# Bidirectional HGRN2 keys from the middle of each chunk, projections and heads in another order, two weight chunks loaded earlier

## The chip, the cores and the metric

The kernel runs on one core of one Trainium2 chip. The metric is the device time of one execution in microseconds (us), median of the runs. TensorE multiplies matrices (PE in the profile, PEld its weight loads), VectorE (DVE) and ScalarE (ACT) work on tiles of 128 partitions, GpSimd (POOL) does little here, and SyncE (SP) only issues DMA transfers.

## What is computed

One encoder layer for 256 tokens of width 1024, in float32: a token mixer, a layer norm, a mixture of 32 experts (top 4 per token), a second layer norm. All weights are read from DRAM once; the experts' are 32 x 12 MB. The change lies in the mixer's recurrence, which runs forwards and backwards over chunks of 32 tokens:

```python
b = jnp.cumsum(logf, axis=3)
b_ref = b[:, :, :, CHUNK // 2 - 1:CHUNK // 2]
b_last = b[:, :, :, CHUNK - 1:CHUNK]
scores = jnp.einsum('bhntd,bhnsd->bhnts', q * jnp.exp(b - b_ref), k * jnp.exp(b_ref - b))
...
kv = jnp.einsum('bhnsd,bhnse->bhnde', k * jnp.exp(b_last - b), v)
decay = jnp.exp(b_last[:, :, :, 0])
def step(S, inp):
    kv_c, dec_c = inp
    return dec_c[..., None] * S + kv_c, S
...
o_inter = jnp.einsum('bhntd,bhnde->bhnte', q * jnp.exp(b), S_prev)
```

## The kernel before

**Steps.** The mixer's matrix products are cut into 64 steps (`run`): 48 for the input projection (24 column blocks of 256, two steps of half the depth each), 8 for the two branch matrices, 8 for the output matrix. A step first splits the weights of the step after next into a rounded copy (`hi`, ScalarE, L233) and the rest (`lo`, VectorE, L234), orders the chunk that comes due (`load_on`), then issues two halves of TensorE work, three groups of four matmuls each (L176: hi, low activations with hi, lo). The copies have three buffers, so a split waits for the step three back. `after` functions (sigmoids, copies of a projection's result) run in the next step.

**Tasks.** What is not a projection is written as generators in `tasks`, each with a first step, and is advanced once in each half step (or in each n-th). `factors(p)` makes, for a pair of heads p, the cumulated decays (`dec`) and from them `qt` and `kt` (queries and keys measured from the chunk's middle), `kd` (keys measured from the chunk's end) and `xx` (queries times the whole decay). `head(h)` makes the scores from `kt` and `qt` (L378), transposes `kd` (L383, `ktp`), copies that to SBUF on ScalarE (L387), multiplies it with the values (L399, `kvp`), runs the recurrence over 8 chunks on VectorE (L409, L412), and sums up on TensorE (L417, L422, `o`); then it normalises (L427 to L434), transposes (L438, `ytp`) and multiplies with the gate. `biases()` splits the experts' biases into three bf16 parts (L514 to L519). Four engines and SP run in the order written (`manual_schedule`), so the place of a task in the steps fixes what stands behind what.

**Chunks.** Weights come in chunks of 1 MB into a ring of slots: pools b (9 slots), c (4), a (4), d (4). The mixer's own chunks use the four a slots. Its intermediate tiles lie in b and c slots (`hold`, `hold_c`), and pool d takes the room of the mixer's operand tiles and is made when they are given up (`mix_ctx.close()`, after the last product with the output matrix). `PF` lists the steps at which a chunk of the first two experts is ordered ahead, one per slot of the ring in turn: 14 in all. After the mixer SP orders every further chunk as its slot falls free. SP works its orders in turn, so one that waits holds up those behind it.

Of the kernel before, what the change touches and what calls it, by code (L numbers as in the profile page):

```python
# [18 lines left out]
P = 128  # L19
T = 256  # L20
# [20 lines left out]
def encoder(ctx: ExitStack, tc: tile.TileContext, x, w_in, conv_w, p_a, lbl, norm_w, p_b, w_o, ln1_g, ln1_b,  # L41
# [136 lines left out]
    def two_parts(hi, lo, src):  # L178
# [6 lines left out]
    cc = hold_c[0][:, 0:512].rearrange("p (i t) -> p i t", i=2)  # L185
    z = hold_c[0][:, 512:1028].rearrange("p (i t) -> p i t", i=2)
    dgs = hold_c[0][:, 1028:1540].rearrange("p (i n e) -> p i n e", i=2, n=NT)
    qT, gwT = (hold_c[1][:, i * 1024:(i + 1) * 1024].rearrange("p (h t) -> p h t", h=NH) for i in range(2))
    sg = [hold_c[2 + q // 2][:, q % 2 * 1024:(q % 2 + 1) * 1024].rearrange("p (i n t) -> p i n t", i=2, n=2)
          for q in range(4)]  # L190
# [3 lines left out]
    xx0, sig1, omf, qt, kt, kd, sig0, lf = [dirs(*n) for n in ((1, 0), (1, 1), (2, 0), (4, 0), (4, 1), (5, 0), (8, 0),  # L194
                                                              (8, 1))]
    sig, xxs = [sig0, sig1], [xx0, sig0]
    dec = half_of(2, 1).rearrange("p (d t) -> p d t", d=2)
    kns = half_of(5, 1).rearrange("p (i d n e) -> p i d n e", i=2, d=2, n=NT)
    Ss = [hold[6 + i].rearrange("p (d c e) -> p d c e", d=2, c=NCH) for i in range(2)]
# [3 lines left out]
    nc.gpsimd.memset(dgs, 0.0)  # L203
    mxh = mxl = None
# [33 lines left out]
    ahead, PF = [], [8, 26, 31, 32, 35, 36, 40, 41, 42, 47, 47, 53, 58, 58]  # L238
# [84 lines left out]
    def factors(p):  # L323
# [23 lines left out]
        blast = bass.AP(tensor=dec.tensor, offset=dec.offset + CH - 1, ap=[p0, [2 * T - CH + 1, 2], [CH, nchk], [0, CH]])  # L347
# [3 lines left out]
        nc.vector.tensor_tensor(four(xx), b4, bref, op=OP.subtract)  # L351
        yield
        nc.vector.tensor_tensor(four(kd), blast, b4, op=OP.subtract)
        yield
        qb = qT[:, None, 2 * p:2 * p + 2, :].to_broadcast([P, 2, 2, T])
        nc.scalar.activation(flat(qt), flat(xx), AF.Exp)
        yield
        nc.scalar.activation(flat(kt), flat(xx), AF.Exp, scale=-1.0)
        nc.vector.tensor_mul(qt, qt, qb)
        yield  # L360
        nc.scalar.activation(flat(kd), flat(kd), AF.Exp)
        nc.vector.tensor_mul(kt, kt, omf)
        yield
        nc.scalar.activation(flat(lf), dec.rearrange("p d t -> p (d t)"), AF.Exp)
        nc.vector.tensor_mul(kd, kd, omf)
        yield
        nc.vector.tensor_mul(xx, lf, qb)
        yield

    def head(h):  # L370
        p, h2 = h // 2, h % 2
        v, qp, eb, dg, kn, S, yb = vs[:, p], xxs[p], lf, dgs[:, h2], kns[:, h2], Ss[h2], ybs[h2]
# [8 lines left out]
        for d in range(2):  # L381
            for tt in range(NT):
                nc.tensor.transpose(kv4[:, d, tt, :], kd[:, d, h2, tt * P:(tt + 1) * P], ident)  # L383
# [18 lines left out]
        for i in range(2):  # L402
            for n in range(4 * i, min(4 * i + 4, NCH - 1)):
                for d in range(2):
# [3 lines left out]
                    if n == 0:  # L408
                        nc.scalar.copy(S[:, d, c + step, :], kv)  # L409
                    else:  # L410
                        last = c * CH + (CH - 1 if d == 0 else 0)
                        nc.vector.scalar_tensor_tensor(S[:, d, c + step, :], S[:, d, c, :],  # L412
                                                       eb[:, d, h2, last:last + 1], kv, op0=OP.mult, op1=OP.add)
            yield
        o = bank("b", "o")[:, 0:NT * P].rearrange("p (n e) -> p n e", n=NT)
# [84 lines left out]
    def biases():  # L500

        def load(src):
            bf = half_of(3, len(bfs) % 2)[0:96]
# [84 lines left out]

    for p in range(2):
# [4 lines left out]
        if p == 0:  # L594
            project(3584, got_g(0))
            project(512, got_c(0))
    project(1024, got_h(0))
    project(0, got_b(0))
    project(512 + H2, got_c(1))
    project(1024 + H2, got_h(1))  # L600
    project(H2, got_b(1))
    project(3584 + H2, got_g(1))
    for q in range(4):
        for i in range(2):
            project(4096 + i * DM + q * H2, got_gate(q, i))
# [602 lines left out]
```

## Time and profile before

| | us |
|---|---|
| median of 3 runs | 1169.03 (1168.68 to 1171.88) |
| the profiled execution | 1167.09, its span 1165.4 |
| TensorE busy in the span | 1074.9 (92%) |
| VectorE busy | 343.8 (30%) |
| ScalarE busy | 224.5 (19%) |
| bytes moved by DMA | 440.39 MB, mean 378 GB/s |

The span is cut by the program into a mixer (to about 227 us), the experts, and a short end. Busy shares are averages over these and say little for one of them; the views by stretch do.

### The profile page before, as it was taken

Reading aid. Unit: us, or ns where it says so; the run is one execution under the profiler, and the core shown is the slowest. Engines: PE = TensorE matmul, PEld = TensorE weight load, DVE = VectorE, ACT = ScalarE, POOL = GpSimd, SP = SyncE. Lnnn points to the kernel's source line nnn. Section 1 sums busy time; section 2 is a strip of 40 time slices with the busy share of each in tenths; the row PEclk is TensorE's granted clock in tenths of the full one; section 3 lists DMA queues with packets and bytes.
Section 4 is the critical chain, followed back from the end, with each engine's and each line's share of the span. In section 5 each row is a group of like instructions: output and inputs, shape, how many; then the busy total and the mean of one; then the engine's idle time right before and its main releaser. Section 6 shows DMA issues by size and latency. Waiting matters only on the chain. (4 is left out here: it accounts for less than half of the span.)

```text
span 1165.4 us, 14653 instructions
## 1 busy us (share of the span) xinstructions
PE 1074.9 (92%) x6176; PEld 544.8 (47%) x6176; DVE 343.8 (30%) x631; ACT 224.5 (19%) x376; POOL 12.4 (1%) x36
## 2 busy tenths in 40 slices
PE   8999999989999999999999898989898999888994
PEld 7899899734343443433343333333333333333344
DVE  5678746621212131313212121212121111111124
ACT  4857444311010101010110101010010001010111
POOL 1000000000000000000000000000000000000001
PEclk9999999999999999999999999999999999999998
DMA  9645597699999999999999999999999999999994
GB/s 295 208 146 169 194 363 273 251 416 423 425 422 425 424 424 425 422 424 424 424 424 424 424 423 424 423 423 425 423 425 423 424 424 424 424 424 425 427 378 127
DMA packets 109701, 440.39 MB, mean 378 GB/s; under 512 B 8224, under 2 KB 41184, under 8 KB 76864
## 3 DMA queue, kind: packets, MB, share of 16 engines
q1 hardware_dynamic: 109440, 439.05, 92.9%
q8 instruction: 50, 0.82, 0.3%
q10 hardware_dynamic: 192, 0.36, 0.1%
q14 instruction: 19, 0.16, 0.0%
HBM read 438.34 MB, written 1.05 MB: 377 GB/s over the span
## 5 line engine op out<-in xcount | busy, mean ns | idle before, releaser
L683 PE MATMUL hb<-ck,xg 128*64 128x512 f32 x2048 | 465.3, 603 | 39.3 <-DMA ck<-in_w_dram 39.3
L683 PEld LDWEIGHTS hb<-ck,xg 128*64 128x64 f32 x2048 | 143.0, 138 | 342.7 <-issue 243.2
L915 PE MATMUL y<-ck,aT 128*64 128x512 f32 x960 | 214.0, 598 | 17.5 <-ACT aT L692 17.4
L659 DVE TENSOR_SCALAR g<-hb 128x512 f32<-128x512 f32 x32 | 22.1, 691 | 658.5 <-PE hb L683 658.5
L915 PEld LDWEIGHTS y<-ck,aT 128*64 128x64 f32 x960 | 66.6, 138 | 152.9 <-issue 119.5
L660 ACT ACTIVATE s<-g 128x512 f32<-128x512 f32 x32 | 20.1, 629 | 557.0 <-DVE g L659 557.0
L234 DVE TENSOR_TENSOR lo<-ck,hi 128x1024 fp32r<-128x1024 f32 x62 | 75.4, 1221 | 53.5 <-ACT hi L233 53.2
L233 ACT CAST hi<-ck 128x1024 fp32r<-128x1024 f32 x62 | 64.3, 1044 | 48.1 <-PE pj L176 38.2
L176 PE MATMUL pj<-xh,hi 128*128 128x256 f32 x352 | 60.2, 295 | 0.8 <-ACT hi L233 0.8
L886 PEld LDWEIGHTS gthp<-oneh,xs 128*128 128x128 f32 x480 | 54.7, 192 | 12.8 <-PE hb L683 8.1
L176 PE MATMUL pj<-xh,lo 128*128 128x256 f32 x352 | 58.5, 290 | 2.0 <-DVE lo L234 2.0
L176 PE MATMUL pj<-xl,hi 128*128 128x256 f32 x352 | 58.6, 290 | 0.0
L927 PE MATMUL cb<-ys,gT 128*128 128x512 f32 x120 | 57.8, 605 | 0.0
L886 PE MATMUL gthp<-oneh,xs 128*128 128x128 f32 x480 | 57.6, 278 | 0.0
L176 PEld LDWEIGHTS pj<-xh,lo 128*128 128x128 f32 x352 | 50.5, 199 | 2.3 <-DVE lo L234 2.2
L176 PEld LDWEIGHTS pj<-xh,hi 128*128 128x128 f32 x352 | 50.4, 199 | 2.0 <-ACT hi L233 1.2
L176 PEld LDWEIGHTS pj<-xl,hi 128*128 128x128 f32 x352 | 50.6, 199 | 0.0
L932 DVE TENSOR_TENSOR acc<-acc,cb 128x512 f32<-128x512 f32 x56 | 35.9, 681 | 7.1 <-PE cb L927 6.8
L921 ACT COPY ys<-y 128x512 f32<-128x512 f32 x30 | 16.1, 589 | 100.2 <-PE y L915 100.2
L816 ACT ACTIVATE xg<-gthp,cols 128x128 f32<-128x128 f32 x60 | 22.6, 456 | 62.0 <-PE gthp L886 62.0
L927 PEld LDWEIGHTS cb<-ys,gT 128*128 128x128 f32 x120 | 20.5, 190 | 27.0 <-issue 11.8
L661 DVE TENSOR_TENSOR g<-g,s 128x512 f32<-128x512 f32 x32 | 22.1, 692 | 25.4 <-ACT s L660 25.4
(250 smaller groups left out, 666.8 us busy)
## 6 DMA issues: line engine op xcount, KB each, us to landing
ck<-in_w_dram SPq DMA_DIRECT2D x380, 1024.0 KB, 19.6
ck<-in_w_in_dram SPq DMA_DIRECT2D x23, 1024.0 KB, 5.5
ck<-in_w_o_dram SPq DMA_DIRECT2D x4, 1024.0 KB, 4.9
ck<-in_w_dram SPq DMA_DIRECT2D x16, 256.0 KB, 5.0
ck<-in_p_a_dram SPq DMA_DIRECT2D x2, 1024.0 KB
ck<-in_p_b_dram SPq DMA_DIRECT2D x2, 1024.0 KB
xs<-in_x_dram SPq DMA_DIRECT2D x2, 512.0 KB
ck<-in_w_in_dram SPq DMA_DIRECT2D x2, 512.0 KB, 6.5
```

What stands on the lines that cost most here:

```text
L176: mm(dst, st, mv, start=start and i == 0, stop=stop and i == len(todo) - 1, skip_group_check=True)
L233: nc.scalar.copy(hi, src)
L234: nc.vector.tensor_tensor(lo, src, hi, op=OP.subtract)
L659: nc.vector.tensor_scalar(g, gl, LIMIT, None, op0=OP.min)
L660: nc.scalar.activation(s, g, AF.Sigmoid, scale=SW_ALPHA)
L661: nc.vector.tensor_tensor(g, g, s, op=OP.mult)
L683: mm(hb[i][ct * 64:(ct + 1) * 64, :], xg[:, k, e2 * CAP:(e2 + 1) * CAP], c1[k][:, lo:lo + 512], start=False, stop=k == NK - 1)
L816: nc.scalar.activation(xg[:, k, :], src, AF.Identity, bias=b1c[:, k:k + 1], scale=g1c[:, k:k + 1])
L886: mm(gp[:, k4 * P:(k4 + 1) * P], zn[:, tt, k * P:(k + 1) * P], oneh[:, tt].rearrange("p e s -> p (e s)"), start=tt == 0, stop=tt == NT - 1)
L915: mm(y[half][ct * 64:(ct + 1) * 64, :], aT[:, j, hh * 64:(hh + 1) * 64], c2[kt // 2][:, kt % 2, half * 512:(half + 1) * 512], start=kt == ...
L927: mm(cb, gT[:, half, tt, :], ys[half], start=True, stop=True)
L932: nc.vector.tensor_add(acc[:, tt, s], acc[:, tt, s], cb)
```

## The change

`factors` no longer makes `kd` nor the exponential of the whole `dec`. `head` transposes `kt` instead of `kd`. The state S is then measured from the middle of the last chunk, and is multiplied at each chunk by `gs`, one factor per chunk and head: the exponential of (end minus middle of the chunk before) plus (middle of this chunk). `xx` becomes `qt` times `gs`. `kt` takes the tile of `lf`.

The projections stand in another order: gates 0 to 2 come after the heads' projections, then the convolution's three for both halves, then gate 3; `gwT` of the second pair comes with that pair. Head 0 starts half a step later (14), head 1 too (16.5); each head has one more empty half step ahead of `o`. `biases` moves from step 8 (every 4th half step) to 28 (every 3rd). In `PF` the 2nd chunk goes from step 26 to 10, the 4th from 32 to 29, others by a few steps. The tiles in `hold` and `hold_c` have other slots.

```diff
-    xx0, sig1, omf, qt, kt, kd, sig0, lf = [dirs(*n) for n in ((1, 0), (1, 1), (2, 0), (4, 0), (4, 1), (5, 0), (8, 0),
-                                                              (8, 1))]
+    xx0, sig1, omf, qt, lf, sig0 = [dirs(*n) for n in ((2, 0), (2, 1), (3, 0), (4, 0), (4, 1), (7, 0))]
+    kt = lf
...
+    gs = mp.tile([P, 2, 2, NCH], F32, name="gs")
+    gr = mp.tile([P, 2, 2, NCH], F32, name="gr")
...
+    nc.gpsimd.memset(gs, 0.0)
...
-    ahead, PF = [], [8, 26, 31, 32, 35, 36, 40, 41, 42, 47, 47, 53, 58, 58]
+    ahead, PF = [], [8, 10, 26, 29, 34, 37, 39, 40, 42, 43, 47, 53, 58, 58]
...
         nc.vector.tensor_tensor(four(xx), b4, bref, op=OP.subtract)
-        yield
-        nc.vector.tensor_tensor(four(kd), blast, b4, op=OP.subtract)
+
+
+        at = lambda i: [dec[:, d].rearrange("p (h c t) -> p h c t", h=2, t=CH)[:, :, :, i if d == 0 else CH - 1 - i]
+                        for d in range(2)]
+        mid, end = at(CH // 2 - 1), at(CH - 1)
+        for d in range(2):
+            nc.vector.tensor_tensor(gr[:, d], end[d], mid[d], op=OP.subtract)
+            now, was = (slice(1, NCH), slice(0, NCH - 1)) if d == 0 else (slice(0, NCH - 1), slice(1, NCH))
+            nc.vector.tensor_tensor(gs[:, d, :, now], mid[d][:, :, now], gr[:, d, :, was], op=OP.add)
+        yield
         yield
         qb = qT[:, None, 2 * p:2 * p + 2, :].to_broadcast([P, 2, 2, T])
+        nc.scalar.activation(gs, gs, AF.Exp)
         nc.scalar.activation(flat(qt), flat(xx), AF.Exp)
         yield
         nc.scalar.activation(flat(kt), flat(xx), AF.Exp, scale=-1.0)
+        yield
         nc.vector.tensor_mul(qt, qt, qb)
         yield
-        nc.scalar.activation(flat(kd), flat(kd), AF.Exp)
         nc.vector.tensor_mul(kt, kt, omf)
         yield
-        nc.scalar.activation(flat(lf), dec.rearrange("p d t -> p (d t)"), AF.Exp)
-        nc.vector.tensor_mul(kd, kd, omf)
-        yield
-        nc.vector.tensor_mul(xx, lf, qb)
+        yield
+        nc.vector.tensor_tensor(four(xx), four(qt), gs.rearrange("p d h c -> p d (h c)")[:, :, :, None]
+                                .to_broadcast([P, 2, 2 * NCH, CH]), op=OP.mult)
         yield
...
-                nc.tensor.transpose(kv4[:, d, tt, :], kd[:, d, h2, tt * P:(tt + 1) * P], ident)
+                nc.tensor.transpose(kv4[:, d, tt, :], kt[:, d, h2, tt * P:(tt + 1) * P], ident)
...
-                        last = c * CH + (CH - 1 if d == 0 else 0)
-                        nc.vector.scalar_tensor_tensor(S[:, d, c + step, :], S[:, d, c, :],
-                                                       eb[:, d, h2, last:last + 1], kv, op0=OP.mult, op1=OP.add)
+                        nc.vector.scalar_tensor_tensor(S[:, d, c + step, :], S[:, d, c, :], gs[:, d, h2, c:c + 1], kv,
+                                                       op0=OP.mult, op1=OP.add)
             yield
+        yield
...
+    gate = lambda q, i: project(4096 + i * DM + q * H2, got_gate(q, i))
     for p in range(2):
         project(1536 + p * H2, got_q(p))
         for d in range(2):
             project(2048 + d * 512 + p * H2, got_f(p, d))
         project(3072 + p * H2, got_i(p), natural=True)
-        if p == 0:
-            project(3584, got_g(0))
-            project(512, got_c(0))
-    project(1024, got_h(0))
-    project(0, got_b(0))
-    project(512 + H2, got_c(1))
-    project(1024 + H2, got_h(1))
-    project(H2, got_b(1))
-    project(3584 + H2, got_g(1))
-    for q in range(4):
+        project(3584 + p * H2, got_g(p))
+    for q in range(3):
         for i in range(2):
-            project(4096 + i * DM + q * H2, got_gate(q, i))
+            gate(q, i)
+    for p in range(2):
+        project(512 + p * H2, got_c(p))
+        project(1024 + p * H2, got_h(p))
+        project(p * H2, got_b(p))
+    for i in range(2):
+        gate(3, i)
...
-    tasks += [[0.5, constants(), 1], [3, load_small(), 2], [7, factors(0), 1], [13.5, head(0), 1],
-              [16, head(1), 1], [20.5, factors(1), 1], [28, head(2), 1], [30.5, head(3), 1], [8, biases(), 4],
+    tasks += [[0.5, constants(), 1], [3, load_small(), 2], [7, factors(0), 1], [14, head(0), 1],
+              [16.5, head(1), 1], [20.5, factors(1), 1], [28, head(2), 1], [30.5, head(3), 1], [28, biases(), 3],
               [44, router_constants(), 2]]
```

What the engines run after it, at three places. VectorE from the second scan of `factors(0)` to the first head's masked scores (`ck` are the mixer's tiles, `sc` the scores, `bsp` the biases' parts), before:

```order
L336 SCALAR_TENSOR_TENSOR ck<-seg,ck 128x512
L234 TENSOR_TENSOR lo<-ck,hi 128x1024
L351 TENSOR_TENSOR ck<-ck 128x1024
L234 TENSOR_TENSOR lo<-ck,hi 128x1024
L353 TENSOR_TENSOR ck<-ck 128x1024
L234 TENSOR_TENSOR lo<-ck,hi 128x1024
L481 SCALAR_TENSOR_TENSOR ck<-ck,cols,pj 128x256 x2
L359 TENSOR_TENSOR ck<-ck 128x1024
L362 TENSOR_TENSOR ck<-ck 128x1024
L234 TENSOR_TENSOR lo<-ck,hi 128x1024
L365 TENSOR_TENSOR ck<-ck 128x1024
L517 TENSOR_TENSOR ck<-ck,bsp 64x1024
```

and now:

```order
L339 SCALAR_TENSOR_TENSOR ck<-seg,ck 128x512
L237 TENSOR_TENSOR lo<-ck,hi 128x1024
L353 TENSOR_TENSOR ck<-ck 128x1024
L360 TENSOR_TENSOR gr<-ck 128x16
L362 TENSOR_TENSOR gs<-ck,gr 128x2x7
L360 TENSOR_TENSOR gr<-ck 128x16
L362 TENSOR_TENSOR gs<-ck,gr 128x2x7
L237 TENSOR_TENSOR lo<-ck,hi 128x1024 x2
L491 SCALAR_TENSOR_TENSOR ck<-ck,cols,pj 128x256 x2
L371 TENSOR_TENSOR ck<-ck 128x1024
L237 TENSOR_TENSOR lo<-ck,hi 128x1024
L373 TENSOR_TENSOR ck<-ck 128x1024
```

The subtraction L353 and the product L365 for `kd` are gone, four small operations have come, a `lo` stands between the products for `qt` (L371) and `kt` (L373), and the biases are no longer among them.

VectorE in `factors(1)`, from its first scan, before:

```order
L334 SCALAR_TENSOR_TENSOR ck<-seg,ck 128x512
L234 TENSOR_TENSOR lo<-ck,hi 128x1024
L455 TENSOR_TENSOR ck<-ck,pj 128x2x256
L336 SCALAR_TENSOR_TENSOR ck<-seg,ck 128x512
L517 TENSOR_TENSOR ck<-ck,bsp 32x1024
L234 TENSOR_TENSOR lo<-ck,hi 128x1024
L462 SCALAR_TENSOR_TENSOR ck<-ck,cols 128x256 x4
L351 TENSOR_TENSOR ck<-ck 128x1024
L353 TENSOR_TENSOR ck<-ck 128x1024
L234 TENSOR_TENSOR lo<-ck,hi 128x1024
L469 TENSOR_TENSOR ck<-ck,pj 128x512
L359 TENSOR_TENSOR ck<-ck 128x1024
```

and now:

```order
L337 SCALAR_TENSOR_TENSOR ck<-seg,ck 128x512
L237 TENSOR_TENSOR lo<-ck,hi 128x1024
L451 TENSOR_TENSOR yb<-ytp,ck 128x256
L339 SCALAR_TENSOR_TENSOR ck<-seg,ck 128x512
L180 TENSOR_TENSOR ybl<-yb,ybh 128x256
L237 TENSOR_TENSOR lo<-ck,hi 128x1024
L353 TENSOR_TENSOR ck<-ck 128x1024
L360 TENSOR_TENSOR gr<-ck 128x16
L362 TENSOR_TENSOR gs<-ck,gr 128x2x7
L360 TENSOR_TENSOR gr<-ck 128x16
L362 TENSOR_TENSOR gs<-ck,gr 128x2x7
L237 TENSOR_TENSOR lo<-ck,hi 128x1024 x2
```

The convolution (L455, L462, L469) and the biases (L517) no longer stand between the scan and the next splits.

ScalarE around the end of head 1 and the start of `factors(1)` (`o` and `yb` are the head's output, `v` the values), before:

```order
L427 ACTIVATE yb,ss<-o 128x128 x2
L233 CAST hi<-ck 128x1024
L320 COPY v<-pj 128x512
L434 ACTIVATE yb<-o,rs 128x128 x2
L329 ACT_TABLE_LOAD
L329 ACTIVATE ck<-ck,lb,oml 128x256 x4
L233 CAST hi<-ck 128x1024
```

and now:

```order
L437 ACTIVATE yb,ss<-o 128x128 x2
L332 ACT_TABLE_LOAD
L332 ACTIVATE ck<-ck,lb,oml 128x256 x4
L236 CAST hi<-ck 128x1024
L444 ACTIVATE yb<-o,rs 128x128 x2
L236 CAST hi<-ck 128x1024
L497 ACT_TABLE_LOAD
```

The table load and the four logarithms of `factors(1)` now come ahead of the scaling of head 1's output (L444), on which its transposes on TensorE wait, and the gates' sigmoids ask for a further table load behind them.

## Rows read from the trace of the kernel before

**Rows 1.** Stretches: us; PE, PEld, DVE, ACT, POOL busy; PEclk, DMA share, GB/s.

```profile
40.00:60.00 20.00, 17.22 (x154) 16.91 (x153) 16.66 (x18) 17.11 (x19) 0.00 (x0) 0.85 0.56 168
100.00:120.00 20.00, 17.96 (x187) 17.33 (x186) 19.80 (x29) 13.62 (x18) 0.38 (x3) 0.91 0.70 232
224.00:228.00 4.00, 3.52 (x18) 2.52 (x17) 3.64 (x11) 1.63 (x3) 0.00 (x0) 1.00 0.00 2
400.00:800.00 400.00, 375.53 (x1814) 146.49 (x1812) 81.08 (x149) 37.67 (x77) 0.00 (x0) 0.99 1.02 424
```

**Rows 2.** Timeline of SP's DMA orders: start, length in us, order.

```profile
209.54 4.50 SPq L70 DMA_DIRECT2D ck<-in_w_dram  x5
...
227.14 1.28 SPq L70 DMA_DIRECT2D ck<-in_w_dram  x3
```

**Rows 3.** Timeline of PE, the last product with the output matrix.

```profile
226.95 0.40 PE L176 MATMUL op<-wo,mxl 128*128 128x512 f32 x1
```

**Rows 4.** PE's waits to 232 us: total, times, longest, in us.

```profile
PE o L422 <- DVE ck L412: 2.2, 2, 2.0
PE pj L176 <- DVE lo L234: 2.0, 1, 2.0
PE ktp L383 <- DVE ck L365: 1.9, 1, 1.9
PE sc L378 <- DVE ck L362: 0.9, 1, 0.9
```

**Rows 5.** Timeline of PE around head 0's scores, up to its `kvp`.

```profile
51.28 0.64 PE L176 MATMUL pj<-xh,lo 128*128 128x256 f32 x4
...
61.18 1.17 PE L399 MATMUL kvp<-v,ck 32*128 32x128 f32 x32
```

**Rows 6.** The same instructions of PE for head 2.

```profile
111.31 0.64 PE L176 MATMUL pj<-xh,lo 128*128 128x256 f32 x4
...
115.73 1.17 PE L399 MATMUL kvp<-v,ck 32*128 32x128 f32 x32
```

**Rows 7.** Timeline of PE in `factors(1)`, projections only.

```profile
101.29 0.64 PE L176 MATMUL pj<-xl,hi 128*128 128x256 f32 x4
...
108.92 0.64 PE L176 MATMUL pj<-xh,hi 128*128 128x256 f32 x4
109.40 0.64 PE L176 MATMUL pj<-xl,hi 128*128 128x256 f32 x4
```

**Rows 8.** Timeline of PE, `o` of head 2, to the next projection.

```profile
121.24 0.38 PE L417 MATMUL o<-v,ck 128*128 128x128 f32 x2
...
126.04 0.72 PE L176 MATMUL pj<-xh,hi 128*128 128x256 f32 x4
```

**Rows 9.** The same instructions of PE for head 0.

```profile
66.70 0.38 PE L417 MATMUL o<-v,ck 128*128 128x128 f32 x2
...
69.29 0.72 PE L176 MATMUL pj<-xh,hi 128*128 128x256 f32 x4
```

**Rows 10.** Timeline of DVE: product for `kt`, convolution, a small product.

```profile
51.53 1.22 DVE L362 TENSOR_TENSOR ck<-ck 128x1024 f32<-128x1024 f32 x1
...
98.61 1.91 DVE L462 SCALAR_TENSOR_TENSOR ck<-ck,cols 128x256 f32<-128x256 f32 x4
...
251.23 0.16 DVE L836 TENSOR_TENSOR e<-mx 128x8 f32<-128x8 f32 x1
```

**Rows 11.** Timeline of ACT: the biases' first cast, and head 1's end.

```profile
44.08 1.05 ACT L514 CAST bsp<-ck 96x1024 bf16<-96x1024 f32 x1 [0.72 <-DMA ck<-in_b_dram]
...
80.50 0.28 ACT L427 ACTIVATE yb<-o 128x128 f32<-128x128 f32 x1 [0.72 <-PE o L422]
...
84.95 0.63 ACT L434 ACTIVATE yb<-o,rs 128x128 f32<-128x128 f32 x2
85.59 1.28 ACT L329 ACT_TABLE_LOAD   x1
86.89 2.08 ACT L329 ACTIVATE ck<-ck,lb,oml 128x256 f32<-128x256 f32 x4
```

More of the change, by code (lines that the diff above doesn't have):

```diff
@@ L184, in encoder @@
     hold_c = [chunks_c.tile([P, 2048], F32, name="ck") for _ in range(NC_)]
[L185 to L188, printed above, removed]
+    qT, gwT = (hold_c[0][:, i * 1024:(i + 1) * 1024].rearrange("p (h t) -> p h t", h=NH) for i in range(2))
+    cc = hold_c[1][:, 0:512].rearrange("p (i t) -> p i t", i=2)
+    z = hold_c[1][:, 512:1028].rearrange("p (i t) -> p i t", i=2)
+    dgs = hold_c[1][:, 1028:1540].rearrange("p (i n e) -> p i n e", i=2, n=NT)
     sg = [hold_c[2 + q // 2][:, q % 2 * 1024:(q % 2 + 1) * 1024].rearrange("p (i n t) -> p i n t", i=2, n=2)
@@ L193, in encoder @@
     dirs = lambda n, i: half_of(n, i).rearrange("p (d h t) -> p d h t", d=2, h=2)
-    xx0, sig1, omf, qt, kt, kd, sig0, lf = [dirs(*n) for n in ((1, 0), (1, 1), (2, 0), (4, 0), (4, 1), (5, 0), (8, 0),
-                                                              (8, 1))]
+    xx0, sig1, omf, qt, lf, sig0 = [dirs(*n) for n in ((2, 0), (2, 1), (3, 0), (4, 0), (4, 1), (7, 0))]
+    kt = lf
     sig, xxs = [sig0, sig1], [xx0, sig0]
-    dec = half_of(2, 1).rearrange("p (d t) -> p d t", d=2)
-    kns = half_of(5, 1).rearrange("p (i d n e) -> p i d n e", i=2, d=2, n=NT)
-    Ss = [hold[6 + i].rearrange("p (d c e) -> p d c e", d=2, c=NCH) for i in range(2)]
+    dec = half_of(3, 1).rearrange("p (d t) -> p d t", d=2)
+    kns = half_of(7, 1).rearrange("p (i d n e) -> p i d n e", i=2, d=2, n=NT)
+    Ss = [hold[5 + i].rearrange("p (d c e) -> p d c e", d=2, c=NCH) for i in range(2)]
+    gs = mp.tile([P, 2, 2, NCH], F32, name="gs")
+    gr = mp.tile([P, 2, 2, NCH], F32, name="gr")
     vs = rt.tile([P, 2, NT, 2, P], F32, name="v", tag="xg")
@@ L346, in factors @@
         bref = bass.AP(tensor=dec.tensor, offset=dec.offset + CH // 2 - 1, ap=[p0, [2 * T + 1, 2], [CH, nchk], [0, CH]])
-        blast = bass.AP(tensor=dec.tensor, offset=dec.offset + CH - 1, ap=[p0, [2 * T - CH + 1, 2], [CH, nchk], [0, CH]])
         flat = lambda z: z.rearrange("p d h t -> p (d h t)")
@@ L371, in head @@
         p, h2 = h // 2, h % 2
-        v, qp, eb, dg, kn, S, yb = vs[:, p], xxs[p], lf, dgs[:, h2], kns[:, h2], Ss[h2], ybs[h2]
+        v, qp, dg, kn, S, yb = vs[:, p], xxs[p], dgs[:, h2], kns[:, h2], Ss[h2], ybs[h2]
         sc = bank("b", "sc")[:, 0:2 * NT * CH].rearrange("p (d n t) -> p d n t", d=2, n=NT)
@@ L502, in load @@
         def load(src):
-            bf = half_of(3, len(bfs) % 2)[0:96]
+            bf = half_of(8, len(bfs) % 2)[0:96]
             for r in range(3):
```

## The prediction

> **What bounds the kernel now.** I first read the view by stretches, to see which resource is full where. From 400 to 800 us the DMA engines are full (share 1.02, 424 GB/s) [rows 1]: the experts' weights come in as one stream, and nothing that is done on the engines there shortens it. What can move is when this stream begins. Between 224 and 228 us DMA carries 2 GB/s [rows 1], so there is something that it waits for, and the second view, SP's orders, names it: five chunks are ordered from 209.54, the next three only from 227.14 [rows 2]. Their slots are made from the mixer's operand tiles, and TensorE starts its last product on these at 226.95 [rows 3]. The stream's begin hangs on the end of the mixer on TensorE, so a microsecond less there is one less at the end, as long as the chunks ordered ahead (14 before, 14 after) have landed.
>
> Third, TensorE's waits in the mixer [rows 4]: four lines, all on VectorE, 7.0 us together. They are not the whole loss. The granted clock is 0.85 on the mean of 40 to 60 us and 0.91 of 100 to 120 [rows 1]: after the two longest pauses there TensorE runs a while at 1.2 GHz in place of 2.4. The reader should take the loss from start to start, against the same instructions where nothing waits.
>
> **What each pause costs.** (a) Head 0's scores: from the last projection group ahead of them to `kvp`, 61.18 - 51.28 = 9.90 us [rows 5]; for head 2 the same takes 115.73 - 111.31 = 4.42 [rows 6]. Loss 5.48, waits and slow clock. (b) In `factors(1)` eight groups take 108.92 - 101.29 = 7.63; one group at full clock takes 109.40 - 108.92 = 0.48 [rows 7], eight 3.84. Loss 3.79. (c) `o` of head 2 with the scores behind it: 126.04 - 121.24 = 4.80 [rows 8], for head 0 69.29 - 66.70 = 2.59 [rows 9]. Loss 2.21. Sum 11.48.
>
> **What the change does to them, step by step.**
>
> (a) TensorE waited for the product for `kt`, which ends at 51.53 + 1.22 = 52.75 [rows 10], then for the one for `kd`. The second is gone: `ktp` now takes `kt`, so it waits for nothing that the scores did not wait for. Head 0 comes half a step later, three groups of 0.48 [rows 7], so TensorE is there at about 51.76 + 1.44 = 53.2 in place of 51.76. Is `kt` ready? On ScalarE the biases' cast with its wait (0.72 + 1.05) [rows 11] goes from ahead of the exponentials; in its place stands the exponential of `gs`, 32 columns, which I bound by nothing and by the 0.28 of 128 columns [rows 11], and take at the upper end. So the exponentials and the split between them come about 1.5 us earlier. On VectorE the product for `kt` gets one `lo` ahead of it, of the same width as itself, 1.2 [rows 10]. Net 52.75 - 1.5 + 1.2 = 52.4, 0.8 ahead of TensorE. The four small operations on 16 columns each: no row has them; between nothing and a full product of 1.22, nearest to the 0.16 of 8 columns [rows 10], so 4 x 0.16 = 0.6, at a point where VectorE has no backlog (they follow the subtraction for `xx`, where the subtraction for `kd`, as wide as the 1.22 product, stood). I count the whole 5.48 as gained; if the cover of 0.8 goes, TensorE waits by as much as it falls short, without the second wait.
>
> (b) The `lo` that TensorE waited for stood behind the convolution's four operations (1.91) [rows 10], the biases' subtraction and the subtractions for `xx` and `kd`. Now gates are projected in these steps, and they want only a sigmoid of ScalarE. Convolution and biases go to steps 28 and later, where no `factors` runs; a step there is six groups, 2.88 us, and one `lo` of 1.2 leaves VectorE 1.7 of it for this work. 3.79 gained.
>
> (c) The second half of the recurrence stood behind a projection's `lo` and the convolution. It stays behind the `lo`, but the convolution is later, and each head has an empty half step (1.44) ahead of `o`. Together more than the wait of 2.0 [rows 4]. 2.21 gained.
>
> New waits. At head 1 the transposes of its output come 12 groups after `o`, 12 x 0.48 = 5.76 us. ScalarE has to do in that time two squares (0.28 each), a table load (1.28), four logarithms (2.08), one `hi` (about the 1.05 of the cast) and the scaling (0.63) [rows 11]: 5.6. Before, the scaling came ahead of the table load. With its waits for semaphores it can be late by nothing to 0.4; I take 0.2. The next row's begin shows that the load holds up no more than its own time: it begins at 85.59 and the logarithm at 86.89, 1.30 later [rows 11]. The Trainium skill (ScalarE: Activation LUTs, What ACT_TABLE_LOAD costs) says otherwise: a switch costs about 1.28 us of load and another 1.38 of drain, 2.66 in all. By it the scaling would be late by 1.4 more and the sum smaller by as much; the trace does not show the drain, so the row's price stands. There is one table load more in the mixer than before, between sigmoids and `gs`, at a place where ScalarE's splits have most of a step in hand.
>
> The two early chunks and the other moves in `PF`: their number up to the end of the mixer is the same, and DMA is at 0.56 and 0.70 in these stretches [rows 1], so they cost nothing and gain nothing as long as DMA has such room; without it each would push a projection's chunk back by one MB, 2.5 us at 424 GB/s. On SP a chunk that waits for its slot holds up the projection chunks behind it. By `load_on` these are ordered when the split four chunks back is done, some six steps of 2.88 us ahead of their own, 17 us; that is the cover. The biases' six transfers and their casts move with the task; their first cast may wait for its transfer as before (0.72), while TensorE has two steps in hand.
>
> **The sum.** 11.48 - 0.2 = 11.3 us. Against the profiled execution: 1167.09 - 11.3 = 1155.8. The median of the runs, 1169.03, lies 1.94 above that execution, so I expect **1157.7** for a median.
>
> **The rivals.**
>
> *Half of it comes back.* The new order packs the second pair's sigmoids, a table load more and the start of `factors(1)` together. If ScalarE falls behind there or at head 0, TensorE meets one pause of some 2.1 us and the slow clock after it. The slow clock cost 9.90 - 4.42 less the waits 0.9 and 1.9 = 2.7 in (a), so with what pauses remain I price it at 2.1 + 2.7 + the 0.7 of a late `kt`: 5.5 given back, 1163.2. For it: ScalarE was busy 17.11 of 20 us there [rows 1] and the cover at two places is under 1 us. Against: it loses two wide exponentials in each `factors`, and the casts of the biases there.
>
> *The gain does not reach the stream* (the change does what it says in the mixer, the end stays): if the stream's begin hung on something else, a late chunk or a slot. Then 1169.0. Against it are the empty 224 to 228 us and the order that follows 0.2 us after TensorE's last product [rows 1 to 3].
>
> *Slower.* The one mechanism that could give more than is saved: ScalarE's copy of the transposed keys. If a backlog of over 2.9 us (two half steps) stands ahead of it when `ktp` is done, `kvp` waits at every head, and the clock falls each time: four times (2.0 + 2.7) = 18.8 against 11.5 saved, 7.3 slower: 1176.3. It decides at the copy's place behind the splits and a gate's sigmoid; nothing in the rows has a backlog of half that once the biases' casts are gone.
>
> **How the numbers follow.** A measurement of this kernel tells 0.3%, 3.5 us, from no change. Chances: forecast 0.71, half back 0.16, no gain 0.08, slower 0.05. The first two are faster by over 0.3%: 0.87; no gain is 0.08; slower 0.05. Range: at the top the second case, 1163.5. At the bottom the scatter (the profiled execution's 1.9 below the median) and what the stream may win besides, if it starts fuller, some 1.5: 1154. That leaves the last two cases out, 0.13, and little at the edges.
>
> **What would show it.** In the profile after: no wait of TensorE over 0.5 us between 10 us and the end of the mixer, in particular none on `sc`, `ktp`, `o` or a `lo`; granted clock 1.00 in the stretches of 40 to 60 and 100 to 120; the three orders after the mixer at about 216 in place of 227.14; the end as far behind them as before (1165.4 - 227.1 = 938.3 us). At head 1 a wait on the scaling of at most 0.4. I am wrong if the orders come at 216 and the end does not follow, or if a wait of 2 us with a slow clock behind it stands at another place, above all between 70 and 100 us on ScalarE's scaling or `hi`.

## The result and the profile after

| | before | after |
|---|---|---|
| median of 4 runs of each on one chip, us | 1168.86 (1168.40 to 1171.88) | 1156.52 (1154.50 to 1157.74) |
| ratio, 95% interval | | 0.9887, 0.9866 to 0.9909 |
| the profiled execution, its span | 1167.09, 1165.4 | 1156.35, 1154.4 |
| SP's three orders after the mixer | 227.14 | 215.88 |

1157.7 was predicted, 1156.52 came. The stretches of the kernel after (us; PE, PEld, DVE, ACT, POOL busy; PEclk, DMA share, GB/s) answer to [rows 1]:

```profile
40.00:60.00 20.00, 20.00 (x218) 19.57 (x218) 17.39 (x27) 15.54 (x21) 0.00 (x0) 1.00 0.71 242
100.00:120.00 20.00, 20.00 (x283) 18.51 (x282) 15.34 (x32) 10.32 (x19) 0.00 (x0) 1.00 1.00 328
213.00:217.00 4.00, 3.39 (x18) 2.43 (x17) 3.61 (x12) 1.37 (x3) 0.00 (x0) 1.00 0.16 25
```

TensorE is busy for the whole of both 20 us and at full clock, where it had lost 2.8 and 2.0 us and run at 0.85 and 0.91. DMA is still nearly empty just ahead of the stream, 11 us sooner. TensorE's waits to 222 us (total, times, longest) answer to [rows 4]; all four of the mixer are gone. What is left lies at the start (the input, the first split) and behind the mixer (`htp`, `rp`):

```profile
PE tp L637 <- DMA xs<-in_x_dram: 4.8, 1, 4.8
PE pj L176 <- ACT hi L236: 0.8, 1, 0.8
PE htp L745 <- DVE xs L735: 0.5, 1, 0.5
PE rp L753 <- ACT hT L746: 0.3, 1, 0.3
```

Head 0 on TensorE, from the last group ahead of the scores to `kvp`, answers to [rows 5]:

```profile
53.15 0.64 PE L176 MATMUL pj<-xh,lo 128*128 128x256 f32 x4
53.72 0.46 PE L388 MATMUL sc<-ck 128*32 128x32 f32 x32
54.11 0.66 PE L393 MATMUL ktp<-ident,ck 128*128 128x128 f32 x4
...
57.56 1.17 PE L409 MATMUL kvp<-v,ck 32*128 32x128 f32 x32
```

It takes 57.56 - 53.15 = 4.41 where it took 9.90 (5.49 won, 5.48 predicted). On VectorE the product for `kt` ends at 51.81 + 1.22 = 53.03, 0.69 ahead of the scores (0.8 predicted):

```profile
50.67 1.22 DVE L237 TENSOR_TENSOR lo<-ck,hi 128x1024 fp32r<-128x1024 f32 x1
51.81 1.22 DVE L373 TENSOR_TENSOR ck<-ck 128x1024 f32<-128x1024 f32 x1
```

The end of the mixer, of TensorE and of SP, answers to [rows 2, 3]:

```profile
215.69 0.40 PE L176 MATMUL op<-wo,mxl 128*128 128x512 f32 x1
215.88 1.28 SPq L70 DMA_DIRECT2D ck<-in_w_dram  x3
```

**How the mixer is handed on.** Near the end SP orders the last expert's pieces (16 orders in a row), then the output. Before, then after:

```profile
1115.81 26.36 SPq L1011 DMA_DIRECT2D ck<-in_w_dram  x16
1158.26 4.19 SPq L1145 DMA_DIRECT2D out_dram<-acc  x3
```

```profile
1103.74 26.86 SPq L1020 DMA_DIRECT2D ck<-in_w_dram  x16
1147.30 4.19 SPq L1154 DMA_DIRECT2D out_dram<-acc  x3
```

From TensorE's last product with the output matrix to the first of these orders it is 1115.81 - 226.95 = 888.86 before and 1103.74 - 215.69 = 888.05 after: this is the stream, and it keeps its length. From that order to the output's it is 42.45 and 43.56: this is a tail that does not.

**The yardstick for the experiments.** TensorE's first six groups take a different time from one execution to the next (last section). So I measure a mixer from the first group of its second projection step to its last product with the output matrix: 226.95 - 14.14 = 212.81 before, 215.69 - 14.67 = 201.02 after, from these rows (before, after) and those above:

```profile
14.14 0.74 PE L176 MATMUL pj<-xh,hi 128*128 128x256 f32 x4
```

```profile
14.67 0.73 PE L176 MATMUL pj<-xh,hi 128*128 128x256 f32 x4
```

By it the change wins 11.79 us of mixer. Of the profiled execution 0.53 of that is lost to the slower start, 0.81 more is won in the stream, 1.11 lost in the tail and 0.22 behind it: 10.74, which is 1167.09 - 1156.35.

### The profile page after: what moved, and what is told of

Read it like the earlier page. It is cut to its first block, busy times and chain, and to the rows that moved or that the text cites. A ratio compares the mean times of both kernels' runs of the same rounds, so it can differ in the third digit from the quotient of the medians.

```text
span 1154.4 us, 14668 instructions
## 1 busy us (share of the span) xinstructions
PE 1070.0 (93%) x6176; PEld 541.7 (47%) x6176; DVE 340.5 (29%) x635; ACT 222.3 (19%) x375; POOL 12.5 (1%) x37
## 3 DMA queue, kind: packets, MB, share of 16 engines
HBM read 438.34 MB, written 1.05 MB: 381 GB/s over the span
## 4 chain that ended last, share of the span: by engine, by line
PE 58%; DMA 38%; ACT 1%; DVE 1%; issue 0%; SPq 0%; POOL 0%; DVEq 0%; POOLq 0%
DMA ck<-in_w_dram 38%; PE hb L692 21%; PE pj L176 12%; PE y L924 10%; PE cb L936 3%; PE gthp L895 2%; PE ab L176 2%; PE op L176 2%; PE yb L1108 1%; PE hb L676 1%; ACT xg L825 1%; PE row_b L877 1%; PE atp L698 0%; PE o L432 0%; PE kvp L409 0%
```

## The experiments

They ran on two chips, where the kernel before took 1169.93 (recurrence alone, order alone, biases at 8, heads earlier) and 1169.41 to 1170.06 (the others) in the median. Every ratio is to the kernel before on the same chip. "Mixer", "stream" and "tail" are the distances just told; each comes from one profiled execution per kernel, the median from all runs.

| kernel | median | ratio, 95% interval | mixer | stream | tail |
|---|---|---|---|---|---|
| before | 1168.86 | 1 | 212.81 | 888.86 | 42.45 |
| recurrence alone | 1168.70 | 0.9988, 0.9973 to 1.0002 | 215.00 | 888.84 | 43.57 |
| order alone | 1159.68 | 0.9918, 0.9901 to 0.9936 | 206.77 | 888.53 | 43.23 |
| recurrence, half steps | 1161.52 | 0.9928, 0.9907 to 0.9950 | 205.32 | 888.51 | 44.88 |
| waits filled | 1172.78 | 1.0032, 1.0018 to 1.0045 | 215.02 | 888.86 | 46.45 |
| after | 1156.52 | 0.9887, 0.9866 to 0.9909 | 201.02 | 888.05 | 43.56 |
| biases at 8 | 1159.11 | 0.9917, 0.9899 to 0.9935 | 205.83 | 888.26 | 43.39 |
| heads earlier | 1156.80 | 0.9891, 0.9871 to 0.9911 | 202.62 | 888.19 | 42.94 |
| no empty half step | 1156.91 | 0.9899, 0.9877 to 0.9920 | 201.68 | 888.56 | 43.06 |
| early chunks back | 1156.39 | 0.9884, 0.9864 to 0.9904 | 201.02 | 889.17 | 45.55 |
| no early chunks | 1170.65 | 1.0011, 0.9999 to 1.0024 | 201.05 | 902.74 | 44.64 |
| work in the mixer | 1166.64 | 0.9972, 0.9958 to 0.9986 | 213.26 | 888.57 | 41.25 |
| work in the experts | 1153.75 | 0.9867, 0.9845 to 0.9889 | 201.02 | 888.65 | 42.84 |
| other start | 1159.12 | 0.9918, 0.9897 to 0.9939 | 201.03 | 888.80 | 47.05 |

Five kernels have a mixer of 201.02 to 201.05: this is TensorE's own work, without a wait.

### The recurrence alone

In the kernel before, with `kt` in a tile of its own:

```diff
-        nc.vector.tensor_tensor(four(kd), blast, b4, op=OP.subtract)
...
+        nc.scalar.activation(gs, gs, AF.Exp)
...
-        nc.scalar.activation(flat(kd), flat(kd), AF.Exp)
...
-        nc.vector.tensor_mul(kd, kd, omf)
...
-                nc.tensor.transpose(kv4[:, d, tt, :], kd[:, d, h2, tt * P:(tt + 1) * P], ident)
+                nc.tensor.transpose(kv4[:, d, tt, :], kt[:, d, h2, tt * P:(tt + 1) * P], ident)
```

> The kernel before with the new recurrence alone: keys measured from the middle, factors per chunk, no third exponential and product; projections, heads, biases and early chunks stay where they were. The theory (three losses of TensorE in the mixer, each handed on to the end one for one): the wait of ktp on the third product, 1.9, is gone, the wait of the scores on kt stays at 0.9 or less, the slow clock behind them goes in whole or in part (0 to 2.7); of the loss in the second factors only the difference between the subtraction that goes (1.2) and the four small operations (0.7) is won, 0.5; the third loss stays. So 2.4 to 5.1 faster than the kernel before: 1163.8 to 1166.5, most likely 1165. Rival, the recurrence is all that counts: 1156.5. Rival, the order is all that counts and this is hidden: 1168.9.

1168.70 beside 1169.93: by the interval between 3.2 faster and 0.2 slower, where 2.4 to 5.1 faster was expected. In the profiled execution (1170.72) the mixer is 2.19 longer. TensorE's waits to 230 us in it, in part:

```profile
PE o L428 <- DVE ck L418: 4.4, 3, 2.3
...
PE sc L385 <- DVE ck L370: 0.9, 1, 0.9
```

The wait at `ktp` is gone and `kvp` of head 0 begins 3.0 sooner, at 58.20 in place of 61.18. But `o` then waits for the recurrence, three times, the first time at head 0:

```profile
58.20 1.17 PE L406 MATMUL kvp<-v,ck 32*128 32x128 f32 x32
...
67.26 0.43 PE L428 MATMUL o<-ck 128*32 128x128 f32 x8 [1.92 <-DVE ck L418]
...
73.81 1.17 PE L406 MATMUL kvp<-v,ck 32*128 32x128 f32 x32
```

The clock falls there (granted 0.91 from 60 to 80), and `kvp` of head 1 comes at 73.81, later than before:

```profile
72.34 1.17 PE L399 MATMUL kvp<-v,ck 32*128 32x128 f32 x32
```

What VectorE does ahead of that `o` (its timeline):

```profile
61.16 1.21 DVE L523 TENSOR_TENSOR ck<-ck,bsp 32x1024 f32<-32x1024 f32 x1
62.30 1.20 DVE L237 TENSOR_TENSOR lo<-ck,hi 128x1024 fp32r<-128x1024 f32 x1
63.43 0.67 DVE L313 TENSOR_TENSOR ck<-ck,pj 128x512 f32<-128x512 f32 x1
64.03 3.17 DVE L418 SCALAR_TENSOR_TENSOR ck<-ck,gs,kvp 128x128 f32<-128x128 f32 x12
```

The recurrence (L418) begins only behind a subtraction for the biases, a split and the queries' product. VectorE was the next bound right behind the wait removed. A part of that is not the recurrence's doing. It begins no sooner than in the kernel before (64.03 for 63.61), though VectorE has a wide subtraction and a product less to do. In this execution the biases' first cast on ScalarE waited 1.85 for its transfer, where it had waited 0.72 [rows 11], and the split that VectorE needs next stood behind it:

```profile
45.53 1.05 ACT L520 CAST bsp<-ck 96x1024 bf16<-96x1024 f32 x1 [1.85 <-DMA ck<-in_b_dram]
```

By an estimate from these two waits, `o` would else have begun some 1.1 sooner.

### The order alone

```diff
+    gate = lambda q, i: project(4096 + i * DM + q * H2, got_gate(q, i))
...
-    tasks += [[0.5, constants(), 1], [3, load_small(), 2], [7, factors(0), 1], [13.5, head(0), 1],
-              [16, head(1), 1], ...
+    tasks += [[0.5, constants(), 1], [3, load_small(), 2], [7, factors(0), 1], [14, head(0), 1],
+              [16.5, head(1), 1], ...
```

> The kernel before with the new order of projections, the later heads 0 and 1 and the empty half step alone; recurrence, biases and early chunks stay as before. The theory: the loss at o (2.2) is gone; in the second factors the convolution's 1.9 is no longer ahead of the split, so that 3.8 falls to about 1; at head 0 the half step (1.44) covers the wait on kt (0.9) and 0.5 of that on the third product, 1.4 of it stays, with or without the slow clock (0 to 2.7). So 6.4 to 9 faster than the kernel before: 1160 to 1162.5. With the recurrence alone this should add up to about the whole gain of 12.3. Rival, the recurrence is all that counts: 1168.9.

The medians differ by 10.25, where 6.4 to 9 was expected; the mixer of the profiled execution is only 6.04 shorter, and where the rest of the 10.25 comes from these runs do not show. The waits at `ktp` and `o` are gone, and (b) is won whole: the eight groups take 105.46 - 101.62 = 3.84. New waits stand at `kvp` and at a `lo`, both of head 0:

```profile
PE kvp L399 <- ACT ck L387: 1.6, 1, 1.6
PE pj L176 <- DVE lo L234: 1.4, 2, 1.1
```

```profile
101.62 0.64 PE L176 MATMUL pj<-xl,hi 128*128 128x256 f32 x4
...
105.46 0.64 PE L176 MATMUL pj<-xh,hi 128*128 128x256 f32 x4
```

That is the mechanism of the slower rival, ScalarE's copy of the transposed keys behind other work, at one head: ahead of the copy stand the third exponential with a table load, two splits, a sigmoid with a table load and a cast of the biases.

### The recurrence with the half steps

The recurrence alone, and

```diff
             yield
+        yield
         o = bank("b", "o")[:, 0:NT * P].rearrange("p (n e) -> p n e", n=NT)
...
-              [13.5, head(0), 1], [16, head(1), 1]
+              [14, head(0), 1], [16.5, head(1), 1]
```

> The kernel before with the new recurrence, heads 0 and 1 half a step later and the empty half step ahead of o; projections, biases and early chunks as before. After the run of the recurrence alone the theory is: what it won at ktp was lost again at o (waits of 1.9 and 2.3 on VectorE's recurrence, where there was one of 2.0), since TensorE came there sooner and VectorE did not. With the empty half steps (1.44 each) these waits fall to 0.9 or less and the clock stays up at head 0; the loss in the second factors (3.3 to 3.8) stays. So 6 to 8 faster than the kernel before: 1162 to 1164. Rival, VectorE's backlog ahead of o (biases, convolution) is longer than the half step: 1166 to 1169. Rival, nothing is lacking but the empty half steps: 1156.5 to 1158.

1161.52, just under the range. With heads 0 and 1 half a step later and a half step more ahead of `o`, the mixer is 7.49 shorter than before. Which of the two half steps does it the run does not separate, and up to 1.7 of its distance to the recurrence alone may be the biases' transfer, for which the first cast waits only 0.15 here. Two waits of up to 1.3 stay at `ktp`, and they end with VectorE's recurrence. `ktp` reads none of its results; by the code it takes the bank of PSUM (five, taken in turn) that held the first `kvp` of the head before, which the recurrence still reads.

The loss in the second factors, which I had expected to stay, is mostly gone. The eight groups of (b) take 102.73 - 98.05 = 4.68, where they took 7.63 before and take 109.67 - 102.77 = 6.90 in the recurrence alone, though convolution and biases are where they were:

```profile
98.05 0.64 PE L176 MATMUL pj<-xl,hi 128*128 128x256 f32 x4
...
102.73 0.64 PE L176 MATMUL pj<-xh,hi 128*128 128x256 f32 x4
```

What changed ahead of them is the order on ScalarE. The table load of `factors(1)` comes right behind the squares of head 1, as in the changed kernel; in the recurrence alone it came only behind a split, a copy and the scaling. With the half steps, then in the recurrence alone:

```profile
80.75 1.28 ACT L332 ACT_TABLE_LOAD   x1
```

```profile
87.08 1.28 ACT L332 ACT_TABLE_LOAD   x1
```

So VectorE has the logarithms, and with them its scans, sooner.

### The waits filled

In the kernel before, for head 0, with 9 ahead of the scores and 18 ahead of `ktp`:

```diff
+            for _ in range(n if h == 0 else 0):
+                nc.tensor.transpose(scb[:, 384:512], ident, ident)
```

> The kernel before with 27 transposes of the identity (0.1 each) on TensorE at head 0: 9 ahead of the scores, 18 ahead of ktp, so that they fill the two waits of 0.9 and 1.9 and shorten neither; the results of them are not used. The theory counts 2.7 of the first loss to the slow clock behind these waits: with no pause the granted clock of 40 to 60 is 1.00, the groups behind them take 0.48 in place of 0.85, and the mixer is through 2.0 to 2.7 sooner: TensorE's last product at about 224.5 in place of 226.95, 1166 to 1168 beside 1170 for the kernel before on this chip. Rival, the clock falls all the same, or the loss is the waits alone: 1170, or later by what the transposes take over the waits.

The price of the slow clock was right, the expected gain wrong. From `ktp` to `kvp` it takes 57.31 - 53.92 = 3.39, where it took 61.18 - 55.16 = 6.02: 2.63 less with the clock at 1.00, 2.7 expected.

```profile
53.92 0.60 PE L391 MATMUL ktp<-ident,ck 128*128 128x128 f32 x4
57.31 1.17 PE L407 MATMUL kvp<-v,ck 32*128 32x128 f32 x32
...
65.06 0.43 PE L430 MATMUL o<-ck 128*32 128x128 f32 x8 [1.51 <-DVE ck L420]
...
71.62 1.17 PE L407 MATMUL kvp<-v,ck 32*128 32x128 f32 x32
```

But again `o` waits (1.51) and the clock falls behind it (0.91 from 60 to 80). This execution had a faster start (first group of the second step at 12.67, not 14.14). Counted from there, `kvp` of head 0 comes 2.40 sooner than in the kernel before, and `kvp` of head 1 already 0.75 later. At `o` of head 2 TensorE waits 2.0 in both kernels, and only here the clock falls behind it. Before, then with the waits filled:

```profile
120.00:140.00 20.00, 17.88 (x231) 15.96 (x230) 14.24 (x38) 9.75 (x22) 0.69 (x1) 1.00 0.61 220
```

```profile
120.00:140.00 20.00, 17.89 (x219) 15.87 (x218) 13.36 (x34) 9.01 (x21) 0.69 (x1) 0.91 0.54 193
```

With that the mixer is 2.21 longer, and the tail of this execution is 4.00 longer too. The median is 0.3% above the kernel before.

### The biases at step 8

```diff
-              [28, biases(), 3]
+              [8, biases(), 4]
```

> The changed kernel with the biases back at step 8, every fourth half step. The theory: their casts stand ahead of the exponentials on ScalarE again, with a wait, 1.05 to 1.8 late, against the 0.7 by which kt is now ahead of TensorE; so the scores wait 0.4 to 1.1, and a slow clock may follow (0 to 2.7): 0.4 to 3.8 slower than the changed kernel, 1157 to 1160.3. Rival, the place of the biases has no part in it: 1156.5.

1159.11, within the range; the intervals of the two kernels overlap, but the mixer is 4.81 longer. The scores wait 0.40 for `kt`, as worked out, but more comes at places that I had not named: a `hi` on ScalarE behind the first cast, which waits 2.25 for its transfer, and `ktp` of head 1, which again waits for the recurrence of head 0:

```profile
48.79 0.74 PE L176 MATMUL pj<-xh,hi 128*128 128x256 f32 x4 [1.16 <-ACT hi L236]
...
54.24 0.46 PE L388 MATMUL sc<-ck 128*32 128x32 f32 x32 [0.40 <-DVE ck L373]
...
65.95 0.63 PE L393 MATMUL ktp<-ident,ck 128*128 128x128 f32 x4 [1.80 <-DVE ck L421]
```

### Heads half a step earlier

```diff
-              [14, head(0), 1], [16.5, head(1), 1]
+              [13.5, head(0), 1], [16, head(1), 1]
```

> The changed kernel with heads 0 and 1 half a step earlier, as before the change. The theory: TensorE comes to the scores 1.44 earlier and waits 0.75 for kt, at one place, not two; if so short a wait leaves the clock alone it costs 0.75 (1157.3), if the clock falls up to 3.4 (1160). Rival, the half step is not needed: 1156.5, with no wait on kt.

The wait is there, 0.8 at the scores, and the granted clock from 40 to 60 stays 1.00. The mixer is 1.60 longer in the profile; the medians differ by 0.3, which tells nothing.

### No empty half step

```diff
             yield
-        yield
         o = bank("b", "o")[:, 0:NT * P].rearrange("p (n e) -> p n e", n=NT)
```

> The changed kernel without the empty half step ahead of o. The theory: at head 0 VectorE's second half of the recurrence stands behind a split, as in the run of the recurrence alone; without the biases' and the convolution's work there TensorE waits 0.5 to 1.4 at o of some heads; a wait of that size left the clock alone in the run with earlier heads. So 0.5 to 2.5 slower than the changed kernel, 1157 to 1159. Rival, the waits at o of the recurrence alone (1.9 and 2.3) come back in full with a slow clock: 1161 to 1163. Rival, the later convolution alone removes them: 1156.5.

At `o` of heads 0 and 2 some 0.2 is lost, the mixer is 0.66 longer, and there is no difference in time. In the changed kernel the empty half step does nothing that the medians can tell; whether it was needed with the old order is not shown, since the run above brought both half steps at once. The last rival held in the time: with convolution and biases in later steps VectorE is in time without it.

### The early chunks

```diff
-    ahead, PF = [], [8, 10, 26, 29, 34, 37, 39, 40, 42, 43, 47, 53, 58, 58]
+    ahead, PF = [], [8, 26, 27, 32, 34, 37, 39, 40, 42, 43, 47, 53, 58, 58]
```

> The changed kernel with the two early chunks back (the second at step 26, the third at 27, the fourth at 32); all else stays. The theory: the early places win nothing, since DMA has room later and stands empty just before the stream begins: 1156.5, within 1. Rival, each of them is a chunk less for the stream, 2.5 each: 1161.5.

1156.39: they win nothing and cost nothing. Then without any in the projections, `PF = [56, 57, 58, 59, 60, 61, 62, 63]`:

> The changed kernel without any early chunk in the projections: eight are ordered at steps 56 to 63, the others after them, so that all stand on SP behind the last chunk of the output matrix (ordered at about 187). The theory (one stream at 424 GB/s; 2.47 per chunk): 17 chunks from 187 are through at 229.0, where the three after the mixer now begin at 217.2, so 11.8 later: 1168.3. Against the two early places this bounds what the whole list is worth. Rival, chunks ahead need only be there ahead of the first expert: 1156.5 to 1159.

14.1 slower, 11.8 expected. The mixer is as short as ever (201.05) and the stream 902.74, 14.7 longer. So chunks ahead are worth their time on DMA, but only once the room ahead of the stream is used up: here all of them were moved behind step 55, and DMA was at 0.98 to 1.02 from 186 us on.

### More work for TensorE, in the mixer and in the experts

```diff
+                if c0 >= 4096 + 3 * H2 and c0 % DM == 3 * H2:
+                    mm3(pv[:, i, :], pairs, h == 0 and i == 0, False)
+                    mm3(pv[:, i, :], pairs, False, h == 1)
```

> The changed kernel with all products of the two projections of the last gates issued twice: 24 groups of 0.48 more on TensorE near the end of the mixer, 11.5; the output counts these gates' arguments twice. The theory (the end stands a fixed time behind TensorE's last product with the output matrix, 940.6 in each of the six profiled executions so far): that product at 227.2, the time 1168.0. Rival, the end hangs on something else in the mixer and has slack: 1157 to 1162.

1166.64, 10.1 above the changed kernel; mixer 12.24 longer, the stream as before (888.57). In the profiled execution the added work passes on to the stream's begin one for one, with a fast start (1.3 sooner at the first scores) and the shortest tail of all on the other side. (The distance of 940.6 in the expectation is 940.1 to 941.3 in those six executions.) And in the experts:

```diff
+        for ct in range(2):
+            bias_mm(hb[0][ct * 64:(ct + 1) * 64, :], e, ct * 512, start=False)
```

> The changed kernel with two more products of the biases (64 x 512, bf16) for each of the 32 experts on TensorE, some 0.2 each, 13 in all, about what the run with more work in the mixer added; the first half of the first layer's bias counts twice. The theory: in the experts TensorE waits for weights, so this fills waits: 1156.5 to 1157.5. Rival, TensorE is busy 92% and is the bound there too: 1169.

1153.75: no loss, mixer and stream as in the changed kernel. Whether the 2.8 below 1156.52 are a gain stays open (the intervals overlap). The added work is less than the 13 I had put down: the row of these products takes 0.82 for six where it takes 0.60 for four in the changed kernel, 0.22 more, 7.0 for all 32 experts. The same engine with more to do: dear in one stage, free in the other.

### An attempt at a faster start

```diff
+        loaded.append(loads[1]())
         load_rows()
         load_on(0)
+        warm = bank("a", "warm")
+        for n in range(16):
+            nc.tensor.transpose(warm[:, n % 4 * P:(n % 4 + 1) * P], ident, ident)
...
+        for n in range(8):
+            nc.tensor.transpose(warm[:, n % 4 * P:(n % 4 + 1) * P], ident, ident)
```

> The changed kernel with two edits at its very start: SP orders the second projection's chunk ahead of the seven small row transfers (it stood behind them and was ordered at 8.99, while DMA was empty from 8.5 to 10.5), and TensorE transposes the identity 16 times while it waits for the input and 8 times ahead of the first projection, results not used. The first six groups there take 0.86 each, the later ones 0.48. If that is a matter of how long TensorE has been at work, they take 0.48 and the third step begins at about 15.7 in place of 17.5; the theory (the end follows the mixer one for one) then gives 1154.5 to 1155. Rival, the groups at the start are slow for another reason: 1156.5, later by at most 1 for the transposes.

The mixer was through at 214.40, 1.29 sooner, and the last expert's orders came 0.54 sooner; yet the median is 1159.12. The rows now come too late for TensorE (1.3 at `cp`), and the tail is 47.05, the longest of all. Two stretches of it:

```profile
1123.00:1128.00 5.00, 2.05 (x22) 0.97 (x17) 0.00 (x0) 1.16 (x2) 0.00 (x0) 1.00 0.99 291
1128.00:1133.00 5.00, 2.64 (x26) 2.64 (x28) 0.28 (x1) 0.26 (x1) 0.00 (x0) 0.52 0.96 281
```

TensorE waits for the last weights and then works on them at a granted clock of 0.52. None of these kernels is shown to beat the changed one.

## Why the prediction was right, and where it was not

**The stream's begin hangs on the mixer's end.** Shown: in thirteen kernels with mixers of 201.02 to 215.02 the stream is 888.05 to 889.17 long, and of 11.5 of added work 10.1 came through in the medians. The orders came at 215.88 (216 predicted), the end of the span 938.5 behind them (938.3).

**(a)** 5.49 for 5.48, and its parts too: kt 0.69 ahead, small operations of 0.18 for 0.16, the exponential of `gs` 0.23 under its bound of 0.28, slow clock 2.63 for 2.7. The cover was as thin as said: a cast of the biases ahead of the exponentials, or half a step, uses it up.

**(b) and (c)** were won in full: the eight groups of (b) take 99.91 - 96.07 = 3.84, no wait is left at `o`, and the mixer is down by 11.79, with 11.48 priced. The reasons were right only in part. In (c), "Together more than the wait of 2.0" credits the empty half step, which the changed kernel doesn't need. In (b) the prediction has one cause, convolution and biases out of the way, and that one is nearly enough: with the heads earlier the table load of `factors(1)` stands behind the scaling again, and the `lo` there waits 0.27. But the early table load, which the prediction counts only as a cost ("I take 0.2"), comes with most of (b) too: with the old order of projections the eight groups take 6.90 without it (recurrence alone) and 4.68 with it (recurrence with the half steps). How the two share (b) in the changed kernel is not separated. In the changed kernel:

```profile
96.07 0.64 PE L176 MATMUL pj<-xl,hi 128*128 128x256 f32 x4
...
99.91 0.64 PE L176 MATMUL pj<-xh,hi 128*128 128x256 f32 x4
```

**What the sum took for granted** is that the three losses are each there to be won. Part of (a) is the product for `kd`; taken away alone, in the kernel before, it brings nothing that the runs can tell, since TensorE then stands at `o`, where VectorE's recurrence is next in line, behind the biases, a split and another product. In the changed kernel all three places were relieved at once, and the sum held. How much the parts depend on each other stays open. By the mixers of the profiled executions they do not add up: 2.19 lost by the recurrence alone, 6.04 won by the order alone, 11.79 by the change. By the medians they nearly do: 1.2, which is not told from nothing, and 10.3, against 12.3. Each of these mixers is one execution: the biases' first cast waited 1.85, 1.16 and 0.72 for its transfer (recurrence alone, order alone, before), and behind `o` of head 2 the clock fell in the first (0.91 from 120 to 140) and not in the other two.

**The wait at head 1** was taken as 0.2, and there is none. ScalarE's scaling ends at 82.98 + 0.61 = 83.59, the transposes begin at 83.86:

```profile
82.98 0.61 ACT L444 ACTIVATE yb<-o,rs 128x128 f32<-128x128 f32 x2
...
84.64 1.28 ACT L497 ACT_TABLE_LOAD   x1
85.94 0.60 ACT L497 ACTIVATE ck<-pj 128x512 f32<-128x512 f32 x1
```

The load is followed 1.30 later by the sigmoid, as in [rows 11]. The Trainium skill (ScalarE: Activation LUTs, What ACT_TABLE_LOAD costs) has 1.38 of drain on top of the load; this trace does not show it either.

**The rivals.** Half back: no pause came. Pauses of that kind can be made (biases at step 8 lose 4.81 of mixer), but the slow clock behind them did not come even there. No gain at the stream: excluded. Slower by the copy of the keys: it occurs once, in the order alone (1.6), with a cast of the biases ahead of the copy, as said, but also with the third exponential and its table load; with the casts alone (biases at 8) `kvp` does not wait.

**The median.** I carried the 1.94 by which the median lay above the profiled execution over to the changed kernel; there the two agree (1156.52 and 1156.35), so 1.77 of it was too much. On the other side the profiled execution won 10.74 and not 11.3, since the slower start and the longer tail took more than the stream gave back. Together that is the 1.2 by which 1157.7 is too high; that the two partly cancel is luck.

## To carry to other kernels

A wait removed is worth its time only up to the next wait on the same engine: before pricing it, move the engine's later work forward by as much and look for who is not ready. Where several such waits lie close together, take away the common work of the engine that is waited for (here the third product, the convolution and the biases on VectorE and ScalarE), or give it more time, and not only one dependency. When an operation moves, ask also what it lets begin sooner: the early table load was priced only for what it holds up. And measure a change by a stretch between two fixed instructions: 201.02 against 212.81 told apart what medians with a scatter of 0.2% could not.

## What was not expected of the hardware

**The start.** Of TensorE's first six groups the first four or more take 0.85 to 1.02 in nine of the fourteen profiled executions, and 0.48 to 0.68 in five (start to start). The view by stretches reads a granted clock of 1.00 there in both, but the first clock entry in the trace, the higher level, comes later than that in the nine: at 13.12 to 14.15 us, and at 5.25 to 8.99 in the five. Ahead of it the 1.00 is no reading. In the nine the groups change to 0.48 just there, and 0.85 is what a group takes at the lower level in the kernel before (58.60 to 59.46 to 60.31, behind the wait at `ktp`). So the slow start is the slow clock. What brings the entry early in five is not shown: the start with transposes ahead has the earliest (5.25), but four come without them.

**The tail.** Between the last expert's first order and the output it is 41.3 to 47.1 us, more than many of the effects studied here. The two longest have the lowest granted clock over the tail, 0.91; the shortest has 0.98. But 44.64 comes with 0.98 too (no early chunks), and 43.23 with 0.93 (order alone), so the clock is not the whole of it. A wait for weights with a slow clock behind it, as in the mixer, is what the longest one shows. What sets it off in one kernel and not in another stays open. The Trainium skill (TensorE: Matmul & The Clock Gate, HAM oscillation) describes such a TensorE, which waits for transfers between short pieces of work and falls back to the lower clock; the row at 0.52 agrees.

**Pauses and the clock.** 0.9 and 1.9 close together bring the clock down (before), one of 1.5 does (waits filled), one of 1.6 does behind a 1.05 and a 0.35 (order alone), one of 1.9 does (`o` of head 0, recurrence alone); one of 0.9 (recurrence alone) or 0.8 (heads earlier) does not, nor does the 1.80 with the biases at 8, where 60 to 80 us reads 1.00. The plainest pair is the 2.0 at `o` of head 2, which brings it down with the waits filled and not in the kernel before, where 120 to 140 us reads 0.91 and 1.00. So the length of a pause alone does not decide it, and a slow clock priced behind a pause, as in the prediction, is a chance and not a certainty.
